# High weight parts that follow a run of 256-column products, stored 192 bytes off a 256-byte line

## The chip, the cores and the metric

The kernel runs on one core of one Trainium2 chip. The metric is the device time of one execution in microseconds (us). Before the change it is 2513.02 us, the median of three runs (2512.54 to 2513.26).

## What is computed

The reference is a small decoder trunk in float32 on a sequence of 256 tokens of width 2048. Layer one is a Mamba-2 mixer, layer two an attention over keys and values made once from the stream. Each mixer is followed by a gated feed-forward block with a short causal convolution, and after every sub-layer the stream is added and normalised. Cut to the matrix products, which hold nearly all of the time:

```python
zxbcdt = x @ w_in                 # 2048 x 10304
mix    = y @ w_out                # 4096 x 2048
u      = causal_dwconv(h @ w_up)  # 2048 x 11264, in each layer
ffn    = (silu(gate) * val) @ w_down   # 5632 x 2048, in each layer
kv     = h @ w_kv                 # 2048 x 4096
q      = h @ w_q                  # 2048 x 2048, and w_o of the same size
```

All weights are streamed once from HBM, about half a gigabyte.

## The kernel before, in words

**Two parts of each number.** Every weight and every activation is cut into a high part (the number rounded to the matrix engine's short float32 form, F32R) and a low part (what is left). A product is the sum of three: high weight by high activation, high weight by low activation, low weight by high activation.

**Steps.** The weights are streamed in 880 steps of 128 partitions x 1024 numbers. A step's tile is loaded by a DMA from SP's queue (`load`, line 179), cut by `split` (lines 182 to 211): ScalarE writes the high part `hi` (line 209), VectorE subtracts and writes the low part `lo` (line 210). There are four `hi` and four `lo` buffers, all in the pool `wts`, so the cutting runs up to four steps ahead of the products.

**Modes.** The steps are grouped into chunks of 512 output columns (`chunks`, line 60). In a chunk of mode W the weights are the stationary operand and the activations stream past them. `some` (line 250) issues the eight products of one step and one part. With the high weights (`p == 0`, line 267) it streams 512 columns, the 256 tokens' high activations and then their low ones (`ch.x.both(k)`). With the low weights (`p == 1`, line 270) it streams only the 256 high ones. In a chunk of mode X the activations are stationary and the weights stream (`half`, lines 231 to 236), 512 columns at a time, or 256 in the last steps of some chunks (`piece`). One small chunk has mode H.

**Order in a W chunk.** A W chunk has 8 steps, in both ways that `cut` (line 82) has of tiling one. `kinds` (line 157) says which part of a step comes first, so that runs of one part join: in the `mamba_w_in` chunks even steps go high, low and odd steps low, high. In all other W chunks ("paired") steps go in twos: high of steps 0 and 1, low of 0 and 1, low of 2 and 3, high of 2 and 3, and so on. So a paired chunk alternates 32 high products and 32 low ones, reaching into the next chunk; a `mamba_w_in` chunk alternates 16 and 16. The very first chunk is `calm` and goes high, low in every step. Other TensorE work (transposes, the scan's and the attention's small products) is put between products at fixed steps by `at`, `amid`, `within` and `beyond`.

**Places within a line.** The code counts addresses in lines of 256 bytes of a partition (`LINE = 64` float32). The activations `hT` and the four `hi` buffers (4096 bytes each) lie on line starts of one common grid. A gap of 192 bytes stands ahead of the four `lo` buffers (4352 bytes each, 17 lines). In W steps the first half of `lo` (the products 0 to 3 of the index order) therefore starts 192 bytes into a line and the second half, 544 numbers further, 64 bytes into one. In X steps both halves are moved up 64 bytes, to a line's start. The low products go through the halves in turn (line 260), the high products first through the first half, then through the second (`order`, line 258).

**What else the diff touches.** `mean` (lines 113 and 598) is the stationary operand of the 16 small products of `z_rms` (line 849); `tri` (line 596) is a mask for `m_cb`. Both lie in the pool `base`, which lives to the end, though only the Mamba layer uses them. The pool `mp` is closed after that layer.

Of the kernel before, what the change touches and what calls it, by code (L numbers as in the profile page):

```python
# [18 lines left out]
F32 = mybir.dt.float32  # L19
F32R = mybir.dt.float32r  # L20
# [4 lines left out]
P = 128  # L25
# [14 lines left out]
NC = 512  # L40
HC = NC // 2
NEG = -1.0e30
LINE = 64
# [16 lines left out]
def chunks():  # L60

    z, b, c, dt = 0, 2 * DI, 2 * DI + NG * DS, 2 * DI + 2 * NG * DS

    def some(mode, name, layer, c0, n, nk):
        return [(mode, name, layer, c0 + i * NC, nk, False) for i in range(n)]

    def ffn(layer):
        up = [some(m, "ffn_w_up", layer, c + j * NC, 1, KD)[0] for j in range(DFF // NC)
              for m, c in (("W" if j else "X", 0), ("W", DFF))]
        return up + some("X", "ffn_w_down", layer, 0, 4, KF)  # L70

    out = some("W", "mamba_w_in", 0, b, 2, KD)
    out[0] = out[0][:5] + (True,)
    out += some("H", "mamba_w_in", 0, dt, 1, KD) + some("W", "mamba_w_in", 0, c, 2, KD)
    for g in range(NG):
        out += some("W", "mamba_w_in", 0, DI + g * NC, 1, KD) + some("W", "mamba_w_in", 0, z + g * NC, 1, KD)
    out += some("X", "mamba_w_out", 0, 0, 4, DI // P) + ffn(0)
    out += some("X", "w_kv", None, D, 1, KD) + some("W", "w_kv", None, 0, 4, KD) + some("W", "attn_w_q", 0, 0, 4, KD)
    return out + some("X", "w_kv", None, D + NC, 3, KD) + some("X", "attn_w_o", 0, 0, 4, KD) + ffn(1)
# [12 lines left out]
def yoco_kernel(ctx: ExitStack, tc: tile.TileContext, x, lmg, lmb, lfg, lfb, x_t, columns, w, out):  # L92
    nc = tc.nc
    base = ctx.enter_context(tc.tile_pool(name="base", bufs=1))
    wts = ctx.enter_context(tc.tile_pool(name="wts", bufs=LA + 1))
# [14 lines left out]

    ident = base.tile([P, P], F32, name="ident")
    make_identity(nc, ident)
    mean = base.tile([P, P], F32R, name="mean")


    cols = base.tile([P, -(-N_COL // LINE) * LINE], F32, name="cols")
# [9 lines left out]
    steps, plan = [], chunks()  # L126
# [45 lines left out]
    def load():  # L172
        i = pos["load"]
        if i >= n_steps:
            return
        pos["load"] += 1
        t = wts.tile([P, 2, NC], F32, tag="raw", name="raw", bufs=RAW)
        for e in (slice(0, 1), slice(1, 2)) if i == 0 else (slice(0, 2),):
            nc.sync.dma_start(t[:, e], w[i][:, e])
        raw_t[i] = t  # L180

    def split():
        i = pos["split"]
        pos["split"] += 1
        t = raw_t.pop(i)
        if i in spare:
            h, l = (bufs["h"][:, k:k + 2].rearrange("p k a t -> p k (a t)") for k in (spare[i], spare[i] + 2))
        else:
            h = wts.tile([P, 2, NC], F32R, tag="hi", name="hi")
            if not gap:  # L190
                gap.append(wts.tile([P, LINE * 3 // 4], F32R, tag="gap", name="gap", bufs=1))
            l = wts.tile([P, 2 * NC + LINE], F32R, tag="lo", name="lo")
            if len(gap) < 2:
                gap.append(wts.tile([P, LINE // 4], F32R, tag="gap2", name="gap2", bufs=1))
            if steps[i][0].mode == "W":
                l = l.rearrange("p (a n) -> p a n", a=2)[:, :, :NC]
            else:
                l = l[:, LINE // 4:LINE // 4 + 2 * NC].rearrange("p (a n) -> p a n", a=2)
        hi_t[i], lo_t[i] = h, l
        if steps[i][0].mode == "H":  # L200
            for a, w in enumerate((h, l)):
                v = t[:, a].rearrange("p (k n) -> p k n", k=8)
                w = w.rearrange("p a (k e n) -> p (a k) e n", e=2, n=NC // 8)
                nc.scalar.copy(w[:, :, 0], v)
                nc.vector.tensor_sub(w[:, :, 1], v, w[:, :, 0].bitcast(F32))
            return load()
        for e in ((0,), (1,)) if i < 2 else ((0, 1),):
            sl = slice(e[0], e[-1] + 1)
            nc.scalar.copy(h[:, sl], t[:, sl])  # L209
            nc.vector.tensor_sub(l[:, sl], t[:, sl], h[:, sl].bitcast(F32))  # L210
        load()

    def splits(i, most=2):

        for _ in range(1 if steps[i][0] in calm else most):
            j = pos["split"]
            ahead = LA + 1 + sum(i <= k < j for k in spare)
            if j < min(i + ahead, n_steps) and (j in spare or sum(k not in spare for k in hi_t) < LA + 1):
                split()
# [333 lines left out]
    def open_pool(name):  # L553
        g = tc.tile_pool(name=name, bufs=1)
        pool[name] = (g, g.__enter__())
        return pool[name][1]
# [26 lines left out]
    calm.append(chB[0])  # L583
    put_x(0)
    split()
    put_x(2)
    split()
    for p in range(2, 8):
        amid(p - 2, put_x, 2 * p)


    mp = open_pool("mamba")
    yT = bufs["y"] = mp.tile([P, DI // P, 2, S], F32R, name="yT")
    BT = mp.tile([P, NG, S], F32, name="BT")
    CT = mp.tile([P, NG, S], F32, name="CT")
    tri = base.tile([P, P], F32, name="tri")
    nc.gpsimd.memset(tri, 1.0 / NC)
    nc.vector.tensor_copy(mean, tri)
    nc.gpsimd.memset(tri, 1.0)
# [530 lines left out]
    for h in range(HEADS):  # L1130
        i, j = divmod(h, 4)
# [87 lines left out]
```

## Time and profile before

| | before |
|---|---|
| median of three runs | 2513.02 us |
| the profiled execution | 2512.1 us |
| its span, first to last instruction | 2509.8 us |
| mean granted TensorE clock | 0.998 |
| high products in W chunks (line 267) | 4480, 128x512 each |
| low products in W chunks (line 270) | 4480, 128x256 each |
| VectorE, ScalarE busy | 66%, 54% |
| DMA | 502.59 MB, mean 200 GB/s |

How to read it: the span is shorter than the execution's time by 2.3 us that lie around the instructions. The profile gives each instruction a start and a duration. Matmuls overlap each other in their pipeline, so a duration is longer than what the instruction costs; what a product costs TensorE in a run of products is the distance from its start to the start of the next one, here called its **pitch**. In the timeline, instructions of one kind that follow each other are merged to one row with its start, length and count. A row that a window cuts counts only the instructions that reach into the window.

### The profile page before, as it was taken

How to read it: one execution, taken by the hardware profiler on the slowest of the kernel's cores; microseconds unless marked ns; L12 is line 12 of the kernel's file. 1: busy time of each engine (PE TensorE's matmuls, PEld its weight loads, DVE VectorE, ACT ScalarE, POOL GpSimd, SP SyncE). 2: the span in 40 equal slices, each digit the busy share in tenths (PEclk: the TensorE clock that was granted, in tenths of full speed). 3: DMA queues.
4: the chain of work that ended last, by engine and by line, in shares of the span. 5: the costliest groups of instructions: out<-in, count | busy, mean ns of one | idle time of the engine just before them, and what ended most of it. 6: DMA issues, size and time to landing. Idle time of an engine off the chain costs nothing.

```text
span 2509.8 us, 36085 instructions
## 1 busy us (share of the span) xinstructions
PE 2497.9 (100%) x13983; PEld 2170.8 (86%) x13983; DVE 1657.9 (66%) x2140; ACT 1365.5 (54%) x1790; POOL 76.4 (3%) x96
## 2 busy tenths in 40 slices
PE   9999999999999999999999999999999999999998
PEld 8888888888888888888888888888888888888887
DVE  7878888755676767675445646645767676765445
ACT  6677787643465655554334445543556555554333
POOL 0000000000200000000000200000200000000001
PEclk9999999999999999999999999999999999999999
DMA  7666655666666556656666665456666556566674
GB/s 260 207 189 205 209 191 190 205 210 220 215 203 193 193 193 193 194 185 202 210 229 204 210 193 175 161 176 227 221 192 197 194 191 194 187 200 201 199 228 161
DMA packets 141739, 502.59 MB, mean 200 GB/s; under 512 B 15856, under 2 KB 16368, under 8 KB 141568
## 3 DMA queue, kind: packets, MB, share of 16 engines
q1 hardware_dynamic: 136448, 482.92, 59.3%
q0 software_dynamic: 4832, 16.85, 2.2%
q8 instruction: 109, 1.79, 0.3%
q14 instruction: 62, 0.51, 0.1%
q10 hardware_dynamic: 288, 0.52, 0.1%
HBM read 491.77 MB, written 8.45 MB: 199 GB/s over the span
## 4 chain that ended last, share of the span: by engine, by line
PE 99%; DMA 0%; DVE 0%; SPq 0%; issue 0%; ACT 0%
PE acc L267 41%; PE acc L270 20%; PE acc L231 11%; PE acc L232 11%; PE acc L236 11%; PE acc L805 1%; PE tp L407 0%; PE tp L236 0%; PE tp L232 0%; PE tp L231 0%; DMA raw<-in_w 0%; PE tp L814 0%; PE acc L788 0%; PE tp L1084 0%; PE tp L1118 0%; PE tp L1110 0%
## 5 line engine op out<-in xcount | busy, mean ns | idle before, releaser
L210 DVE TENSOR_TENSOR lo<-raw,hi 128x1024 fp32r<-128x1024 f32 (+1 forms) x869 | 1060.0, 1225 | 722.6 <-ACT hi L209 596.4
L209 ACT CAST hi<-raw 128x1024 fp32r<-128x1024 f32 (+1 forms) x869 | 909.0, 1049 | 826.8 <-PE acc L236 366.6
L267 PE MATMUL acc<-hT,hi 128*128 128x512 f32 x4480 | 1059.0, 391 | 0.4 <-DVE hT L570 0.3
L267 PEld LDWEIGHTS acc<-hT,hi 128*128 128x128 f32 x4480 | 826.9, 188 | 165.0 <-ACT hi L209 0.9
L270 PEld LDWEIGHTS acc<-hT,lo 128*128 128x128 f32 x4480 | 538.6, 188 | 15.6 <-issue 1.2
L270 PE MATMUL acc<-hT,lo 128*128 128x256 f32 x4480 | 544.6, 277 | 0.0
L232 PE MATMUL acc<-lo,gT 128*128 128x512 f32 (+1 forms) x678 | 254.5, 378 | 0.0
L231 PE MATMUL acc<-hi,gT 128*128 128x512 f32 (+1 forms) x678 | 254.1, 377 | 0.0
L236 PE MATMUL acc<-hi,gT 128*128 128x512 f32 (+1 forms) x678 | 200.7, 377 | 0.0
L232 PEld LDWEIGHTS acc<-lo,gT 128*128 128x128 f32 x678 | 127.7, 188 | 23.3
L231 PEld LDWEIGHTS acc<-hi,gT 128*128 128x128 f32 x678 | 127.6, 188 | 23.1
L236 PEld LDWEIGHTS acc<-hi,gT 128*128 128x128 f32 x678 | 124.9, 188 | 23.6
L232 PE MATMUL acc<-lo,yT 128*128 128x512 f32 (+1 forms) x270 | 98.6, 369 | 0.0
L231 PE MATMUL acc<-hi,yT 128*128 128x512 f32 (+1 forms) x270 | 98.5, 369 | 0.0
L231 PE MATMUL acc<-hi,hT 128*128 128x512 f32 x192 | 78.8, 410 | 0.0
L236 PE MATMUL acc<-hi,yT 128*128 128x512 f32 (+1 forms) x270 | 77.7, 369 | 0.0
L232 PE MATMUL acc<-lo,hT 128*128 128x512 f32 x192 | 75.4, 393 | 0.0
L610 DVE TENSOR_TENSOR u<-u,acc 128x512 f32<-128x512 f32 x108 | 73.5, 681 | 2.3 <-ACT u L609 1.4
L637 DVE SCALAR_TENSOR_TENSOR g<-u,cols,g 128x254 f32<-128x254 f32 (+1 forms) x176 | 73.3, 478 | 2.4 <-ACT g L632 2.4
L1034 ACT CAST gT<-v 128x512 fp32r<-128x512 f32 x44 | 27.3, 621 | 84.5 <-DVE v L1033 84.5
L637 DVE SCALAR_TENSOR_TENSOR v<-u,cols,v 128x254 f32<-128x254 f32 (+1 forms) x176 | 73.2, 478 | 0.0
L469 POOL TENSOR_TENSOR rs<-rs,mhalf 128x1 f32<-128x1 f32 x8 | 7.4, 930 | 1982.1 <-DVE nb L470 1982.1
(223 smaller groups left out, 1911.3 us busy)
## 6 DMA issues: line engine op xcount, KB each, us to landing
raw<-in_w SPq DMA_DIRECT2D x880, 512.0 KB, 3.8
mA<-acum_d POOLq DMA_DIRECT2D x16, 512.0 KB, 6.1
hres<-r POOLq DMA_DIRECT2D x12, 512.0 KB, 7.1
r<-hres SPq DMA_DIRECT2D x12, 512.0 KB, 4.6
eA<-acum_d POOLq DMA_DIRECT2D x16, 128.0 KB, 7.5
r<-in_x SPq DMA_DIRECT2D x4, 512.0 KB, 5.8
gb<-in_ln_mix_g SPq DMA_DIRECT2D x8, 256.0 KB, 4.7
gb<-in_ln_mix_b SPq DMA_DIRECT2D x8, 256.0 KB, 4.9
```

Source lines behind the costliest of these rows:

```text
L209: nc.scalar.copy(h[:, sl], t[:, sl])
L210: nc.vector.tensor_sub(l[:, sl], t[:, sl], h[:, sl].bitcast(F32))
L231: nc.tensor.matmul(a, th, h[:, kk, sl], start=k == 0, stop=False)
L232: nc.tensor.matmul(a, th, l[:, kk, sl], start=False, stop=False)
L236: nc.tensor.matmul(a, ch.x.lo(k)[:, ts], h[:, kk, sl], start=False, stop=k == ch.nk - 1)
L267: nc.tensor.matmul(banks[j], w[:, a, b, js], ch.x.both(k), start=begins, stop=ends, skip_group_check=True)
L270: nc.tensor.matmul(banks[j][:, :S], w[:, a, b, js], ch.x.hi(k), start=begins, stop=ends, skip_group_check=True)
L469: nc.gpsimd.tensor_tensor(self.rs[:, h, :], self.rs[:, h, :], mhalf[:, 0, :], op=OP.pow)
L610: nc.vector.tensor_add(dst, dst, p[:, :, :S])
L637: nc.vector.scalar_tensor_tensor(d, u[:, i % 2, :S - k], c1(self.at_w, w[n - 1 - k] + self.ia + i), d, op0=OP.mult, op1=OP.add)
L805: nc.tensor.matmul(ps[64 * q:64 * q + 64, c, j * P:(j + 1) * P], G[g]["xdt"][:, c, h * 64:(h + 1) * 64], G[g]["A", c][:, h, :], start=True ...
L1034: nc.scalar.copy(h, v[:, sl])
```

## The change

`behind(i)` picks the W steps whose high products are issued right after low products, of the same step or of the step ahead. For a pair only the first of the two steps is picked. For a picked step the first half of `hi` starts 192 bytes into a line; the second half starts on a line. All other steps keep both halves of `hi` on line starts. For this the `hi` buffers grow by one line of 256 bytes each, 1024 bytes in all. To make room, `mean` and `tri` (512 bytes each) move from `base` to `mp`. No instruction is added, removed or put in another order.

```diff
+    def behind(i):
+        ch, s = steps[i]
+        if ch.mode != "W" or (ch.paired and s % 2):
+            return False
+        if ch.kinds(s)[0] == 1:
+            return True
+        ch, s = steps[i - 1]
+        return i > 0 and ch.mode == "W" and ch.kinds(s)[1] == 1
...
-            h = wts.tile([P, 2, NC], F32R, tag="hi", name="hi")
+            h = wts.tile([P, 2 * NC + LINE], F32R, tag="hi", name="hi")
+            if behind(i):
+                h = h[:, LINE // 2:].rearrange("p (a n) -> p a n", a=2)[:, :, LINE // 4:]
+            else:
+                h = h[:, :2 * NC].rearrange("p (a n) -> p a n", a=2)
...
-    mean = base.tile([P, P], F32R, name="mean")
...
-    tri = base.tile([P, P], F32, name="tri")
+    tri = mp.tile([P, P], F32, name="tri")
+    mean = mp.tile([P, P], F32R, name="mean")
```

The arithmetic of the slice: 32 numbers are skipped, the remaining 1056 are cut in two of 528, and of each the first 16 are skipped. So the halves start at numbers 48 and 576 of the buffer, bytes 192 and 2304, and 2304 is nine lines.

## The prediction

> **What bounds the kernel now.** I read the page first: is there an engine that never rests, and does the chain that ended last stay on it?
>
> ```profile
> span 2509.8 us, 36085 instructions
> ...
> PE 2497.9 (100%) x13983; PEld 2170.8 (86%) x13983; DVE 1657.9 (66%) x2140; ACT 1365.5 (54%) x1790; POOL 76.4 (3%) x96
> ...
> PE 99%; DMA 0%; DVE 0%; SPq 0%; issue 0%; ACT 0%
> PE acc L267 41%; PE acc L270 20%; PE acc L231 11%; PE acc L232 11%; PE acc L236 11%; PE acc L805 1%; PE tp L407 0%; PE tp L236 0%; PE tp L232 0%; PE tp L231 0%; DMA raw<-in_w 0%; PE tp L814 0%; PE acc L788 0%; PE tp L1084 0%; PE tp L1118 0%; PE tp L1110 0%
> ...
> L267 PE MATMUL acc<-hT,hi 128*128 128x512 f32 x4480 | 1059.0, 391 | 0.4 <-DVE hT L570 0.3
> ...
> L270 PE MATMUL acc<-hT,lo 128*128 128x256 f32 x4480 | 544.6, 277 | 0.0
> ```
>
> TensorE is the bound from the first microseconds to the last: 99% of the chain. Next, the view of who waited for whom, for TensorE alone: does it ever stand still for weights?
>
> ```profile
> engine line waited for: us in total, times, longest us
> PE tp L582 <- POOL ident masks.py:199: 1.4, 1, 1.4
> PE acc L267 <- DVE hT L570: 0.3, 1, 0.3
> ```
>
> It does not: 1.7 us in all, at the start. So only a shorter pitch of products saves time, and whatever shortens a pitch counts in full. About 0.2% of the time, 5.0 us, is what a measurement of this kernel can tell from no change; that is the bound I use for "same".
>
> Now the pitch, in the timeline of TensorE around one run of 32 high products and the low runs on both sides, in the first layer's feed-forward. The rows come from windows that begin at different products, so that the starts inside a run can be seen.
>
> ```profile
> 771.80 3.45 PE L270 MATMUL acc<-hT,lo 128*128 128x256 f32 x29
> 775.08 7.44 PE L267 MATMUL acc<-hT,hi 128*128 128x512 f32 x32
> ...
> 776.24 0.39 PE L267 MATMUL acc<-hT,hi 128*128 128x512 f32 x1
> ...
> 782.36 3.80 PE L270 MATMUL acc<-hT,lo 128*128 128x256 f32 x32
> ...
> 782.71 3.45 PE L270 MATMUL acc<-hT,lo 128*128 128x256 f32 x29
> ...
> 786.00 7.44 PE L267 MATMUL acc<-hT,hi 128*128 128x512 f32 x32
> ```
>
> The reader is to see starts, not lengths. The high run begins at 775.08; its product number 5 (counting from 0) starts at 776.24; the low run begins at 782.36. The last 27 high products take 782.36 - 776.24 = 6.12 us, **226.7 ns** each. The first five take 1.16 us, 232 ns each. So a high run that comes behind low products pays 1160 - 5 x 226.7 = **26.7 ns** at its head, and nothing later. The low runs do the same on a smaller scale: 29 of them take 775.08 - 771.80 = 3.28 us, 113.1 ns each, and the first three of the next run 350 ns, 350 - 3 x 113.1 = 10.7 ns more than three steady ones.
>
> The view by source line over the same run gives durations without rounding to 10 ns; the first row is of a window over the first four products, the second over the last 27.
>
> ```profile
> L267 PE MATMUL acc<-hT,hi x4: 389/394/397, 775.3 to 776.0; 128*128 128x512 f32 x4
> ...
> L267 PE MATMUL acc<-hT,hi x27: 388/389/389, 776.2 to 782.1; 128*128 128x512 f32 x27
> ```
>
> At the head they last up to 397 ns, then 388 or 389, all 27. The head's loss is real and regular, in the long runs and in the runs of 16 of the Mamba layer:
>
> ```profile
> 351.33 3.81 PE L267 MATMUL acc<-hT,hi 128*128 128x512 f32 x16
> 354.98 1.99 PE L270 MATMUL acc<-hT,lo 128*128 128x256 f32 x16
> 356.81 3.81 PE L267 MATMUL acc<-hT,hi 128*128 128x512 f32 x16
> 360.46 1.99 PE L270 MATMUL acc<-hT,lo 128*128 128x256 f32 x16
> ```
>
> Here 16 high products take 3.65 us against 16 x 226.7 ns = 3.627: again some 23 ns over.
>
> **Is it the low weights' place that causes it?** The tails of the X chunks answer. There 256-column products are followed by 512-column ones with every operand on a line start:
>
> ```profile
> 641.00 0.28 PE L232 MATMUL acc<-lo,yT 128*128 128x256 f32 x1
> 641.12 0.28 PE L231 MATMUL acc<-hi,yT 128*128 128x256 f32 x1
> 641.24 0.28 PE L232 MATMUL acc<-lo,yT 128*128 128x256 f32 x1
> 641.36 0.40 PE L236 MATMUL acc<-hi,yT 128*128 128x256 f32 x2
> 641.60 0.40 PE L231 MATMUL acc<-hi,yT 128*128 128x512 f32 x1
> 641.83 0.40 PE L232 MATMUL acc<-lo,yT 128*128 128x512 f32 x1
> 642.07 0.39 PE L231 MATMUL acc<-hi,yT 128*128 128x512 f32 x1
> 642.29 0.40 PE L232 MATMUL acc<-lo,yT 128*128 128x512 f32 x1
> 642.53 0.62 PE L236 MATMUL acc<-hi,yT 128*128 128x512 f32 x2
> 642.98 0.28 PE L231 MATMUL acc<-hi,yT 128*128 128x256 f32 x1
> ```
>
> Two things stand here. Six 512-column products behind 256-column ones take 642.98 - 641.60 = 1.38 us, 20 ns over six steady ones: the head loss comes with the change of length, wherever the operands ahead lay. And the 256-column products with aligned operands have a pitch of 120 ns, the low products of W chunks, whose stationary operand lies 192 or 64 bytes off, one of 113.1 ns. These differ in more than the place (which operand is the weight), yet it is the nearest evidence that a shifted stationary operand spares a product of 256 columns about 7 ns.
>
> **The change, part by part.**
>
> *Steps picked.* Outside the calm chunk there are 19 chunks of `mamba_w_in` in mode W with four picked steps each (1, 3, 5, 7): 76. There are 50 paired chunks (21 + 21 of the two up-projections, 8 of keys and queries) with two each (2 and 6): 100. The calm chunk has 7, and the step behind it 1. Together **184 steps**. With 70 W chunks x 8 steps x 8 products the sum is the 4480 of the page's row, so no run is missed.
>
> *What can go.* 184 x 26.7 ns = **4.9 us** if each head becomes steady. That is the whole of what stands at these places, 0.195% of the time.
>
> *What stays.* The trace shows no high part at 192 bytes. Bounds: the nearest row is the head of a low run, where shifted weights come behind a change of length, and that pays 10.7 ns; I take this as the remainder, 26.7 - 10.7 = 16 ns gained per step. The far end on the good side is a head without loss in which the four shifted products also save the 7 ns that aligned and shifted 256-column products differ by: 26.7 + 4 x 6.9 = 54 ns, 10.0 us in all. The far end on the bad side is those 7 ns with the other sign on top of today's head, 27.6 ns lost per step, 5.1 us in all. One row speaks against the bad end: the last of the 27 products above has the first shifted low part loaded beside it, and none of the 27 is longer than 389 ns.
>
> *The second half.* Product 4 and its followers return to line starts. Today the loss runs through the fifth product, so one might start afresh there. I take the remainder of 10.7 ns to hold this too; the case that all of it returns is a rival.
>
> *ScalarE and VectorE* now write and read `hi` at another place. Bounds: the subtraction already writes its result shifted in W and aligned in X steps.
>
> ```profile
> L210 DVE TENSOR_TENSOR lo<-raw,hi x30: 1210/1226/1228, 1300.7 to 1382.9; 128x1024 fp32r<-128x1024 f32 x30
> ...
> L210 DVE TENSOR_TENSOR lo<-raw,hi x48: 1216/1225/1227, 761.7 to 889.2; 128x1024 fp32r<-128x1024 f32 x48
> ```
>
> The medians are 1226 ns in X (first row) and 1225 in W. So I cost these edits at nothing. Were it a few ns, TensorE's row of waits shows that nothing of it reaches the end; cover is the two engines' idle third and half.
>
> *`mean` and `tri`* move by whole lines; 16 small products read `mean`, and at 7 ns each even a changed place is 0.1 us. No DMA, queue or wait changes.
>
> **Sum.** 184 x 16 ns = 2.9 us. The profiled execution took 2512.1 us (span 2509.8 and 2.3 around it) and would take 2509.2. It lies 0.9 us under the median of the three runs, so for the median: 2513.0 - 2.9 = **2510.1 us**.
>
> **A page against the change.** The row first: the X and W products of 256 columns differ, 120 to 113 ns. The Trainium skill, "TensorE: Matmul & The Clock Gate", section "Part 2: What happens when you issue a matmul", gives TensorE two independent read ports, one for the streamed and one for the loaded operand, and "SBUF — State Buffer", section "SBUF: two separate sides", says that PE never waits on anyone. By that rule the place of a weight could change no pitch and the sum would be 0; this trace does not bear it out as it stands, since some 7 ns need another cause. Its time is that of the first rival.
>
> **Rivals.**
> 1. *Nothing comes of it.* Either the address plays no part in the head, or the loss only moves: products 0 to 3 run steadily, and the aligned second half then pays the 26.7 ns. For: the X tails show the head loss in the same size whichever low place went ahead; the loss settles only while 512-column products with aligned weights run. Against: 113 to 120 ns. Time 2513.0 us; chance 0.21.
> 2. *The shift is wrong for long products.* Aligned weights are the good place in a steady high run (226.7 ns, no excess), and the bad one in a steady 256-column run (120). If the preference turns with the length, each of the four shifted products pays about 7 ns, and then the aligned half still pays its head: 184 x 27.6 ns = 5.1 us, **2518.1 us**; with half of the four hit, 2515.6. It decides from the point where the four shifted products and the return together cost more than 26.7 ns over steady. Against: the products behind a low run are not in the steady state, and the row of 27. Chance 0.27, mostly between 2513.5 and 2518.
> 3. *More than the head.* The shifted products also drop below 226.7 ns, as the short ones did: up to 10.0 us, 2503.0. Against: the 27th product beside a shifted load is not shorter by 7 ns (388, the minimum, against 389). Chance 0.05.
>
> **How the numbers follow.** The forecast, some of the head gone (gain 1.5 to 4.9 us, 2508.1 to 2511.5), has 0.47. The range reaches from 2508.0 to 2516.5: it leaves out rival 3 and the far part of rival 2, together under 0.2. The cases of a gain and of a loss both hold much: the forecast's own range is 2508.1 to 2511.5. Faster by over 5.0 us needs all of the head and more: 0.08. Slower by over 5.0 us needs rival 2 in full: 0.09. The rest, 0.83, is within 0.2%.
>
> **What would show it.** In the timeline the first five products of a high run behind a low one go from 1.16 us to about 1.14, and the 32 from 7.28 (775.08 to 782.36) to about 7.26; the runs of 16 from 3.65 to 3.63. Low runs (3.64 us for 32) and the X tails (1.38 us) stay as they are: if these move too, it is not the picked steps. In rival 1 the durations over 389 ns move from the products 0 to 4 to the products 3 to 8. In rival 2 the 32 take over 7.28 us. The prediction is wrong if TensorE comes to wait for weights, or if unpicked products change.

## The result, and the profile after

The changed kernel takes **2509.13 us** (median of 20 runs, 2508.64 to 2510.64), the kernel before, run beside it, 2512.96 us (median of 20, 2512.45 to 2513.77). That is 3.83 us less; the ratio is 0.9985 with a 95% interval of 0.9979 to 0.9991. So it is faster, by less than the 0.2% that the prediction set as the bound of "same", and the forecast of 2510.1 us was 1.0 us too high.

The page of the changed kernel, its lines on span, TensorE and the chain. The high products of W chunks are now on line 280, the low ones on line 283.

```profile
span 2506.7 us, 36085 instructions
...
PE 2493.7 (99%) x13983; PEld 2170.5 (87%) x13983; DVE 1658.3 (66%) x2140; ACT 1365.1 (54%) x1790; POOL 76.4 (3%) x96
...
PE 99%; DMA 0%; DVE 0%; SPq 0%; issue 0%; ACT 0%
```

Nothing has changed in kind: TensorE is still the whole chain, with the same 13983 products. The view of waits says the same: TensorE stands still twice, at the start, 2.8 us in all, where it was 1.7.

```profile
PE tp L595 <- POOL ident masks.py:199: 1.4, 1, 1.4
PE acc L280 <- ACT hi L222: 1.4, 1, 1.4
```

The second row is a wait for weights, which the prediction named as a sign of being wrong. It is a single one, ahead of the second step of the kernel, and the third step starts at 12.77 us, where it started at 12.41 before. The shift is not its cause: e1 below leaves the shift out and waits 1.7 us for `hi` ahead of the first two steps. Whether the larger buffers and the moved tables cause it, or one execution differs from the next, no run separates; e1 takes as long as the kernel before, so it costs nothing that these times show.

The timeline of TensorE around a run of 32 high products in the same feed-forward; the third row is of a window that opens where only product 4 and its followers are left.

```profile
759.22 3.80 PE L283 MATMUL acc<-hT,lo 128*128 128x256 f32 x32
762.86 7.42 PE L280 MATMUL acc<-hT,hi 128*128 128x512 f32 x32
...
763.77 6.51 PE L280 MATMUL acc<-hT,hi 128*128 128x512 f32 x28
...
770.12 3.80 PE L283 MATMUL acc<-hT,lo 128*128 128x256 f32 x32
773.75 7.42 PE L280 MATMUL acc<-hT,hi 128*128 128x512 f32 x32
```

The run from 762.86 to 770.12 takes 7.26 us, where it took 7.28. Its last 28 products take 770.12 - 763.77 = 6.35 us, 226.8 ns each: the settled pitch is untouched, and what went is at the head. The low runs take what they took, 3.64 us from 759.22 to 762.86. The view by source line over the first five products and over 26 of the others:

```profile
L280 PE MATMUL acc<-hT,hi x5: 388/390/395, 762.9 to 763.8; 128*128 128x512 f32 x5
...
L280 PE MATMUL acc<-hT,hi x26: 388/389/390, 764.2 to 769.9; 128*128 128x512 f32 x26
```

Before, durations at the head went up to 397 ns with a median of 394; now one or two products still stand out, and the median is 390. Product by product, from the starts in the trace (medians over the 100 picked paired steps, ns over the settled 226.7):

| product | 0 | 1 | 2 | 3 | 4 | 5 and on | sum of 0 to 4 |
|---|---|---|---|---|---|---|---|
| before | 6.3 | 9.3 | 1.3 | 5.3 | 4.3 | 0.3 | 26.5 |
| after | -0.7 | 2.3 | 5.3 | 0.3 | 0.3 | 0.3 | 7.5 |

The starts are whole nanoseconds, so each median is good to about 1 ns. The mean over all picked steps whose first 16 high products follow low ones and run without interruption (153 of the 184) is sharper: these 16 take 26.5 ns more than settled ones before and 6.5 after.

So 19 to 20 ns went in each of 184 steps, 3.5 to 3.7 us; the measured 3.8 has an interval of 2.3 to 5.3 us (0.09% to 0.21% of 2513). The runs of 16 went as the prediction said, from 3.65 to 3.63 us:

```profile
350.51 3.79 PE L280 MATMUL acc<-hT,hi 128*128 128x512 f32 x16
354.14 1.98 PE L283 MATMUL acc<-hT,lo 128*128 128x256 f32 x16
```

Unpicked places did not move: the six 512-column products in the tail of the X chunk take 641.70 - 640.32 = 1.38 us as before.

```profile
640.32 0.40 PE L244 MATMUL acc<-hi,yT 128*128 128x512 f32 x1
...
641.70 0.28 PE L244 MATMUL acc<-hi,yT 128*128 128x256 f32 x1
```

### The profile page after: what moved, and what is told of

It reads as the page before. It is cut to its first block, busy times and chain, and to the rows that moved or that the text cites. A ratio compares the mean times of both kernels' runs of the same rounds, so it can differ in the third digit from the quotient of the medians.

```text
span 2506.7 us, 36085 instructions
## 1 busy us (share of the span) xinstructions
PE 2493.7 (99%) x13983; PEld 2170.5 (87%) x13983; DVE 1658.3 (66%) x2140; ACT 1365.1 (54%) x1790; POOL 76.4 (3%) x96
## 4 chain that ended last, share of the span: by engine, by line
PE 99%; DMA 0%; DVE 0%; SPq 0%; issue 0%; ACT 0%
PE acc L280 41%; PE acc L283 20%; PE acc L245 11%; PE acc L244 11%; PE acc L249 11%; PE acc L819 1%; PE tp L420 0%; PE tp L249 0%; PE tp L245 0%; PE tp L244 0%; PE tp L828 0%; PE acc L802 0%; PE tp L1098 0%; PE tp L1132 0%; DMA raw<-in_w 0%; PE tp L1124 0%
```

## The experiments

The theory is that the place of the first products' weights within their line makes the gain (A). The rivals: the new stride and the moved tables make it (B); any place off a line start would (C); and, on how it works, that a counted state decides when the return to line starts is free (D) or that only the first few products matter (E). All kernels do the same arithmetic.

**e1_room_only: the room without the shift.**

```diff
-            if behind(i):
-                h = h[:, LINE // 2:].rearrange("p (a n) -> p a n", a=2)[:, :, LINE // 4:]
-            else:
-                h = h[:, :2 * NC].rearrange("p (a n) -> p a n", a=2)
+            h = h[:, :2 * NC].rearrange("p (a n) -> p a n", a=2)
```

> The changed kernel with larger buffers and with mean and tri moved, but with both halves of every high part on line starts. Theory A (the place of the first half within its line makes the gain): time as before, 2513.0 us within 0.7, and the head of a high run behind a low one costs 26 to 28 ns again. Theory B (the gain comes from the buffers' new stride and the moved tables): 2509.1 us and heads of about 7 ns, as in the changed kernel.

Measured: 2512.84 us against 2512.79 before, ratio 1.0001 (0.9992 to 1.0010). In the timeline a run of 32 high products takes 783.00 - 775.72 = 7.28 us again:

```profile
775.72 7.44 PE L277 MATMUL acc<-hT,hi 128*128 128x512 f32 x32
783.00 3.80 PE L280 MATMUL acc<-hT,lo 128*128 128x256 f32 x32
```

Theory B falls. The stride of 17 lines and the other place of `hT`, `mean` and `tri` cost and bring nothing that these times can show.

**e2_both_halves: the second half shifted too.**

```diff
-                h = h[:, LINE // 2:].rearrange("p (a n) -> p a n", a=2)[:, :, LINE // 4:]
+                h = h[:, LINE * 3 // 4:LINE * 3 // 4 + 2 * NC].rearrange("p (a n) -> p a n", a=2)
```

> In the picked steps both halves lie 192 bytes into a line; everything else as in the changed kernel. Theory A1 (shifted weights suit only the first products, and in the settled run the line start is the better place): slower than the changed kernel, since products 4 to 7 pay some ns each or the next step pays the head of up to 27 ns; 2510 to 2515 us. Theory A2 (shifted is at least as good anywhere): the same as the changed kernel or up to 4 x 7 ns x 184 = 5 us faster, 2504 to 2509 us.

Measured: 2513.57 us against 2512.79, ratio 1.0003 (0.9994 to 1.0012). The whole gain is gone. The timeline of one run; the second row opens at product 8, the third at product 16:

```profile
765.33 7.45 PE L280 MATMUL acc<-hT,hi 128*128 128x512 f32 x32
...
767.17 5.61 PE L280 MATMUL acc<-hT,hi 128*128 128x512 f32 x24
...
768.99 3.79 PE L280 MATMUL acc<-hT,hi 128*128 128x512 f32 x16
...
772.62 3.80 PE L283 MATMUL acc<-hT,lo 128*128 128x256 f32 x32
```

Eight settled products take 8 x 226.7 ns = 1.81 us. The first eight take 1.84, the next eight, which are the step behind and lie on line starts, 1.82; the last sixteen 3.63, settled. So the shifted second half pays, and the return is paid in the step behind, in all 7.29 us against 7.28 before. A1 holds: that the second half goes back to the line start is part of why the change works.

**e3_all_first: the first half shifted in every W step.**

```diff
-            if behind(i):
+            if steps[i][0].mode == "W":
```

> The first half of every high part in W steps is shifted by 192 bytes, not only behind low products. Rival 2 of the prediction in its general form (a shifted weight costs a settled product of 512 columns about 7 ns): the 376 steps not picked pay up to 4 x 7 ns each, 10.5 us, 2519.6 us. If the place does not matter in a settled run: 2509.1 us as the changed kernel. If it saves there too: down to 2499 us.

Measured: 2519.87 us against 2512.79, ratio 1.0026 (1.0015 to 1.0037), 10.7 us over the 2509.13 of the changed kernel (timed beside another set of runs of the kernel before, 2512.96). The run of 32 takes 772.82 - 765.48 = 7.34 us; the second line is of the view by source line over its last 16 products, where the settled maximum was 389 ns:

```profile
765.48 7.50 PE L280 MATMUL acc<-hT,hi 128*128 128x512 f32 x32
772.82 0.40 PE L283 MATMUL acc<-hT,lo 128*128 128x256 f32 x2
```

```profile
L280 PE MATMUL acc<-hT,hi x16: 388/392/397, 769.1 to 772.6; 128*128 128x512 f32 x16
```

In a settled run the shift does harm, and the sum fits rival 2: 376 unpicked steps at 26.4 ns are 9.9 us. Yet not by its mechanism. From the starts (medians of paired steps, ns over 226.7), beginning with the product beside which the first shifted weight is loaded: -0.7, 2.3, 5.3, -0.7, 9.3, 1.3, 5.3, 4.3. The four shifted loads cost 6 ns together, not four times 7; the other 20 come with the return to the line start.

**e4_scan_heads: sixteen places.** The first half starts `o` bytes into a line.

```diff
             if behind(i):
-                h = h[:, LINE // 2:].rearrange("p (a n) -> p a n", a=2)[:, :, LINE // 4:]
+                o = LINE // 16 * (pos["n"] % 16)
+                o2 = NC + o if pos["n"] // 16 % 2 else NC + LINE
+                pos["n"] += 1
+                h = [h[:, o:o + NC], h[:, o2:o2 + NC]]
...
+        if isinstance(h, list):
+            for a in range(2):
+                nc.scalar.copy(h[a], t[:, a])
+                nc.vector.tensor_sub(l[:, a], t[:, a], h[a].bitcast(F32))
...
```

> In picked steps the first half starts 0, 16, 32 ... 240 bytes into a line in turn, 16 picks with the second half on a line start, then 16 with the second half right behind the first, so at the same place in its line; cut and written half by half. Read by head from the starts of the products. Theory A: the head's loss depends on the place, 27 ns at 0 and about 7 at 192 with the second half on a line start, and other places lie between or above, in a regular order. Theory C (any place off the line start does): about 7 ns at all of 16 to 240 bytes. Time in all between 2509 and 2516 us.

One execution, 2516.16 us, just over the expected 2509 to 2516, beside 2512.79 before; it is read by its heads alone. For each place, the time of the 16 high products from the picked step on, less 16 settled ones, in ns (medians of 3 to 6 undisturbed picks, nearly all within 2 ns; at 144, 192 and 208 one pick lies 4 to 7 ns off):

| bytes into the line | 0 | 16 | 32 | 48 | 64 | 80 | 96 | 112 | 128 | 144 | 160 | 176 | 192 | 208 | 224 | 240 |
|---|---|---|---|---|---|---|---|---|---|---|---|---|---|---|---|---|
| second half on a line start | 26 | 46 | 50 | 44 | 33 | 36 | 55 | 67 | 15 | 31 | 70 | 29 | **6** | 55 | 55 | 33 |
| second half at the same place | 26 | 73 | 77 | 71 | 59 | 36 | 75 | 86 | 75 | 58 | 70 | 42 | 33 | 62 | 82 | 26 |

The timeline at 0, 128, 160 and 192 bytes, each with the row of product 0 and that of product 16:

```profile
831.63 0.63 PE L293 MATMUL acc<-hT,hi 128*128 128x512 f32 x2
835.28 0.39 PE L293 MATMUL acc<-hT,hi 128*128 128x512 f32 x1
...
919.10 0.62 PE L293 MATMUL acc<-hT,hi 128*128 128x512 f32 x2
922.74 0.39 PE L293 MATMUL acc<-hT,hi 128*128 128x512 f32 x1
...
940.93 0.63 PE L293 MATMUL acc<-hT,hi 128*128 128x512 f32 x2
944.63 0.39 PE L293 MATMUL acc<-hT,hi 128*128 128x512 f32 x1
...
962.81 0.62 PE L293 MATMUL acc<-hT,hi 128*128 128x512 f32 x2
966.44 0.39 PE L293 MATMUL acc<-hT,hi 128*128 128x512 f32 x1
```

The reader is to see the distances 3.65, 3.64, 3.70 and 3.63 us, where 16 settled products take 3.63. Theory C falls: of the 16 places only 128 and 192 are better than the line start with room to spare, and most are worse. Theory A's two values came, 26 at 0 and 6 at 192; the regular order of the other places that it expected is not there. In the first column the second half lay one line further in one row than in the other, and both give 26: a whole line more does not matter.

**e5_scan_count: how many products are shifted.** The first `n` products of a step lie 192 bytes into a line, the others on line starts.

```diff
-            if behind(i):
-                h = h[:, LINE // 2:].rearrange("p (a n) -> p a n", a=2)[:, :, LINE // 4:]
+            ch, s = steps[i]
+            if behind(i) or (ch.mode == "W" and ch.paired and s % 4 == 0):
+                q = "n" if behind(i) else "m"
+                c = P * (pos[q] % 9)
+                pos[q] += 1
+                h = [(h[:, LINE * 3 // 4:LINE * 3 // 4 + c], slice(0, c)), (h[:, LINE + c:], slice(c, 2 * NC))]
...
```

> Of each picked step's eight high products the first n are shifted by 192 bytes, n going 0 to 8 in turn; the same n in the paired steps 0 and 4, which begin in a settled high run. Theory D (a counted state: each shifted weight loaded in a long run moves it on by one of three positions that cost -0.7, 2.3 and 5.3 ns, and the return to the line start is free from one position only): behind low products the return is free after n = 4 and 7, so the step costs 6 to 8 ns at 4 and about 14 at 7, and 20 to 30 at the other n; in a settled run free after 3 and 6 (7 and 14 ns) and about 21 ns dearer at the others. Theory E (only the first few products matter and any later return is free): behind low products the cost falls from 27 ns at n = 0 to about 7 at some n and stays there or grows slowly; in a settled run about 2 to 3 ns per shifted product with no jumps.

One execution, 2514.01 us, beside 2512.62 before. Again the time of 16 high products from the picked step on, less 16 settled ones, in ns, read in the feed-forward's runs, where each `n` repeats within 1 ns:

| n | 0 | 1 | 2 | 3 | 4 | 5 | 6 | 7 | 8 |
|---|---|---|---|---|---|---|---|---|---|
| behind low products | 26 | **-1** | 20 | 26 | 6 | 26 | 32 | 12 | 32 |
| in a settled high run | -1 | 20 | 27 | 7 | 27 | 33 | 13 | 33 | 40 |

The timeline for n = 0, 1, 4 and 7 behind low products, the rows of product 0 and of product 16:

```profile
764.65 4.04 PE L305 MATMUL acc<-hT,hi 128*128 128x512 f32 x17
768.30 3.82 PE L305 MATMUL acc<-hT,hi 128*128 128x512 f32 x16
...
775.60 4.02 PE L305 MATMUL acc<-hT,hi 128*128 128x512 f32 x17
779.22 3.83 PE L305 MATMUL acc<-hT,hi 128*128 128x512 f32 x16
...
808.36 4.03 PE L305 MATMUL acc<-hT,hi 128*128 128x512 f32 x17
812.00 3.81 PE L305 MATMUL acc<-hT,hi 128*128 128x512 f32 x16
...
841.15 4.03 PE L305 MATMUL acc<-hT,hi 128*128 128x512 f32 x17
844.79 3.82 PE L305 MATMUL acc<-hT,hi 128*128 128x512 f32 x16
```

The distances are 3.65, 3.62, 3.64 and 3.64 us. Theory D gave the jumps: behind low products the cost is small at 4 and 7, in a settled run at 0, 3 and 6, always three apart, and each round of three adds about 7 ns (-1, 6, 12, or -1, 7, 13). E falls. D missed **n = 1**, where it expected 20 to 30: it is the same series one round earlier, 1, 4, 7. Shifting the first product alone leaves no loss at all. In this scan the n-th weight always lies 512 bytes behind the one before it, so count and address go together; that the free counts are 1, 4, 7 behind low products and 3, 6 in a settled run, with the weights at the same offsets in a step's buffer, speaks for the count.

**e6_low_aligned: the low parts on line starts.** In the changed kernel the low parts of W steps are put where X steps have them.

```diff
-            if steps[i][0].mode == "W":
-                l = l.rearrange("p (a n) -> p a n", a=2)[:, :, :NC]
-            else:
-                l = l[:, LINE // 4:LINE // 4 + 2 * NC].rearrange("p (a n) -> p a n", a=2)
+            l = l[:, LINE // 4:LINE // 4 + 2 * NC].rearrange("p (a n) -> p a n", a=2)
```

> The changed kernel with the low parts of W steps on line starts too (as in X steps). By the row that the prediction leaned on (256-column products with aligned operands have a pitch of 120 ns, not 113): 4480 low products pay 6.9 ns more, 30.9 us, less the head of the low runs, which goes: about 2539 us. If the 120 ns of the X tails has to do with the weights streaming there and not with the place: 2509 us. The head of the high runs: 7 ns as in the changed kernel, if it does not depend on where the low parts lay.

Measured: 2535.71 us against 2512.62, ratio 1.0092 (1.0075 to 1.0109), 26.6 us over the changed kernel's 2509.13 and 3 us less than the 2539 that was expected. The timeline, the second row opening three products into the low run:

```profile
767.21 4.00 PE L280 MATMUL acc<-hT,lo 128*128 128x256 f32 x32
...
767.56 3.64 PE L280 MATMUL acc<-hT,lo 128*128 128x256 f32 x29
...
771.04 7.42 PE L277 MATMUL acc<-hT,hi 128*128 128x512 f32 x32
778.30 4.00 PE L280 MATMUL acc<-hT,lo 128*128 128x256 f32 x32
```

29 low products take 771.04 - 767.56 = 3.48 us, 120 ns each, where shifted ones take 113. The gap is 6.7 ns, not 6.9, and by the starts the first aligned product behind a high run takes 113 as well, not 120, which is most of why the sum was too high. So the row of the X tails that the prediction leaned on does speak of the place. The high run from 771.04 to 778.30 takes 7.26 us, as in the changed kernel: the head does not depend on where the low parts lay.

**e7_first_only and e8_changed_again: the first product alone, beside the changed kernel.** The second has no edit.

```diff
             if behind(i):
-                h = h[:, LINE // 2:].rearrange("p (a n) -> p a n", a=2)[:, :, LINE // 4:]
+                c = P
+                h = [(h[:, LINE * 3 // 4:LINE * 3 // 4 + c], slice(0, c)), (h[:, LINE + c:], slice(c, 2 * NC))]
...
```

> In the picked steps only the first product's 128 columns of high weights are shifted by 192 bytes, the other seven products' are on line starts; the piece is cut by instructions of its own (three instead of one on ScalarE and VectorE in 184 steps). Theory D, with the scan by count (n = 1 leaves no loss at all at the head): the heads go from 27 ns to 0, 184 x 27 = 4.9 us under the kernel before and 1.2 us under the changed one, 2507.8 us. If the scan's heads were so low only because the steps around them differed: heads of 7 to 27 ns and 2509 to 2513 us. If the added instructions on ScalarE and VectorE delay the cutting: idle time of TensorE before the high products, and over 2509 us.

> The changed kernel once more, beside the run that shifts only the first product, so that both are compared on one chip. 2509.1 us, heads of about 7 ns.

Measured on one chip: before 2512.78 us, the changed kernel 2509.49 (ratio 0.9988, 0.9978 to 0.9997), the first product alone **2507.94** (0.9982, 0.9973 to 0.9991). The medians differ by 1.55 us where 1.2 were expected; the intervals overlap, so the times alone do not separate the two, but the profiles do. The timeline and the view by source line of one run of 32, all of it:

```profile
762.54 7.42 PE L302 MATMUL acc<-hT,hi 128*128 128x512 f32 x32
769.80 0.28 PE L305 MATMUL acc<-hT,lo 128*128 128x256 f32 x1
```

```profile
L302 PE MATMUL acc<-hT,hi x32: 388/389/389, 762.5 to 769.6; 128*128 128x512 f32 x32
```

No product lasts over 389 ns; there is no head any more. Over the 153 uninterrupted picked steps the first 16 products take 0.2 ns less than settled ones on average, and 6.5 ns more in e8, as in the changed kernel. The 734 added instructions on ScalarE and VectorE do not show: TensorE waits 1.5 us for ScalarE, in two places at the start, about what the changed kernel does.

```profile
PE tp L617 <- POOL ident masks.py:199: 1.4, 1, 1.4
PE acc L302 <- ACT hi L233: 1.0, 1, 1.0
PE acc L302 <- ACT hi L227: 0.5, 1, 0.5
```

## Why the prediction was right, point by point

*The bound and what stood to be gained.* TensorE as the only bound, a saved nanosecond of pitch as a saved nanosecond of time, 184 steps, and 26.7 ns at each head (26.5 by the starts of 153 heads): all held. The kernel with the first product alone shifted takes the whole 4.9 us (2512.78 to 2507.94, 4.84).

*The remainder.* The term that was mis-sized. I took 10.7 ns for what would stay, from the head of a low run, and so 16 ns gained; 6.5 stayed and 20 were gained. 184 x 4 ns = 0.7 us of the 0.9 by which the gain was put too low. The low run's head was the nearest row but no copy of this one.

*The direction.* It rested on an analogy: shifted weights spare a 256-column product 7 ns, so they should help here too. For 256-column products this is so (e6). For 512-column products in a settled run the sign is the other one (e3), so the analogy alone would have pointed the wrong way. The change pays because the first weights behind low products meet another state, which the prediction named only as an argument against rival 2. That part of its success is luck.

*The second half.* That the return to line starts costs nothing was an assumption put inside the remainder, and it was right by more luck than reason: the count of shifted products decides. With two, three or five shifted products instead of four, 20 to 26 ns would have stayed of the 26, and rival 1 would have been the result.

*Rival 1, nothing comes of it.* Its two forms are both refuted where the change stands (the room alone brings nothing, the place does), but its second form, a loss that only moves, is what happened with both halves shifted. The row that was to speak for it, the X tails, shows 20 ns and not 26.7, so "the same size" was a generous reading.

*Rival 2, the shift is wrong for long products.* Right in a settled run, where the 26.5 ns per step are close to the 27.6 that it named, and wrong in why: a shifted product costs 2.3 ns on average over a round of three, and the return the rest. The products right behind a low run are not in the settled state, which is what the prediction set against it.

*Rival 3* did not come: in the rows shown no product lasts under 388 ns, the settled minimum.

*The row that spoke against the bad end* (27 products, none over 389 ns, the last with a shifted low part loaded beside it) was weak evidence. The load it showed is the first in the round of three, the one that costs -0.7; the two behind it cost 2.3 and 5.3.

*The page against the change.* The Trainium skill, "SBUF — State Buffer", section "SBUF: two separate sides", has PE never waiting. The runs do not agree, as far as that is meant for the place of PE's own two operands: the changed kernel (2509.1 us) and e6 (2535.7) differ in nothing but that place.

## What to carry to other kernels

Where TensorE bounds the kernel, read the pitch product by product around every change of the streamed length, not only its mean: here 27 ns sat in the first five of 32 products, and the mean duration of the high products on the page is 391 ns with them and 390 in e7 without. Where a weight lies within a 256-byte line can set that pitch, but the good place depends on the products around it, so scan places and counts step by step inside one kernel, where each step of the trace is a measurement, before a layout is chosen. Move as little as does the work: one of eight weights was enough, and moving all eight lost everything.

## What the runs showed of the hardware that was not expected

The pitch behaves as if a state behind it were counted, in threes. From a settled run of 512-column products, each weight loaded 192 bytes off moves it by one of three positions that cost -0.7, 2.3 and 5.3 ns; going back to line starts is free after three or six and costs about 20 ns more otherwise, at the next four products (9.3, 1.3, 5.3, 4.3). Behind a run of 256-column products the series is the same, with the free counts at one, four and seven. The same 9.3, 1.3, 5.3 and 4.3 ns are also the last part of the head before the change, so the head looks like such a return. What it is in the chip that is counted stays open; no run looked below the pitch, and only 192 bytes was scanned by count. One whole line more did not matter. And 256-column products differ by 7 ns with the place of their weights (120 and 113 ns), in their settled state, while 512-column ones settle at 226.7 ns with weights on a line start.
